# A two-layer trunk on one core: deeper ring, parts made earlier, and a hand order on ScalarE

## The chip, the cores and the metric

The kernel runs on one core of a Trainium2 chip. The metric is device time in microseconds (us), the median of several runs. The engines are TensorE (PE, its weight loads PEld), VectorE (DVE), ScalarE (ACT), GpSimd (POOL) and SyncE (SP), which here issues the transfers (DMA).

## The reference

256 tokens of 1024 float32 values go through two layers. Each layer is a mixer and a PEER expert retrieval, each followed by a layer norm over the residual:

```python
for i in range(2):
    m = mla(x) if i == 0 else dsa(x)
    x = layernorm(ALPHA * x + m, ln_gain[i, 0], ln_bias[i, 0])
    f = peer(x, w_q[i], sub_keys[i], w_down[i], w_up[i])
    x = layernorm(ALPHA * x + f, ln_gain[i, 1], ln_bias[i, 1])
```

`mla` is attention with low-rank queries, keys and values; `dsa` is attention in which an indexer picks 64 keys for each query. Both have 8 heads of 128. PEER is:

```python
q = (x @ w_q).reshape(T, 8, 2, 128)          # 8 heads, two halves
s1, s2 = scores of each half against its 128 sub-keys
v1, i1 = top_k(s1, 16); v2, i2 = top_k(s2, 16)
best, pos = top_k(v1[:, :, :, None] + v2[:, :, None, :], 16)
expert = i1 * 128 + i2 at pos; gate = softmax(best)
a = x . w_down[expert]                        # 16384 experts of 1024
y = sum over the chosen of gelu(a) * gate * w_up[expert]
```

## The kernel before, in words

**Weights in blocks.** All weights are cut into 604 blocks of 128x1024 float32 (512 KB), numbered in the order of use: 0 to 22 for `mla`, 23 to 38 for the first layer's query weights of PEER, 39 to 166 `down`, 167 to 294 `up`, 295 to 331 for `dsa` (its query heads are 308 to 315, its key heads 316 to 323), then 332 to 347, 348 to 475 and 476 to 603 for the second PEER. PEER computes the hidden unit of every expert for every token and multiplies it with a gate matrix that is zero where the expert was not chosen, so that no rows are gathered.

**High and low parts.** A float32 product is made of float16 parts: ACT makes the high part `hi` of a block (`Split.high`, L89), DVE the low part `lo` (`Split.low`, L98), and PE adds three products: hi by the high part `xh` of x, hi by its low part `xl`, and lo by `xh`. In some stretches one block in three or four is "pooled" (`Stream._pooled`): ACT scales the raw block in place (L164), casts it (L166), and POOL subtracts (L168).

**The stream.** `Stream` (L101) carries the blocks. A raw block is loaded into one of 6 slots of the pool `raws` by SP (L133), its two parts go into rings of `RING` = 6 slots each. `get` takes a block and splits up to `AHEAD` = 3 blocks further; it also loads `DMA_AHEAD` = 5 beyond these. `open` and `close` are the same in two halves, for the places where highs and lows are placed by hand: `open` makes the high part of the next block, `close` its low part. A slot is free once its last reader is done, so a load waits for the low part of an earlier block.

**Order.** Where nothing is said, a scheduler decides the order of each engine's queue from the program. Some of it is set by hand: `queue` (from `queue_of`) chains instructions of an engine in the order of the calls, and `chains[engine]` does so with everything that passes through `pe`, `dve` or `act`; `ws.act = act` puts the stream's own highs into ACT's chain. Each engine executes its queue in order.

**Ends of stages.** `finish` (L472) ends a stage. It takes the last output blocks, normalises the two token tiles (class `Norm`: sums L418, square L426, centre L431, scale L436 and L438, result L443), turns them on PE (class `Turned`, L459, tile names `xt`), splits them into `xh` and `xl`, and begins the next stage's matmuls in row form with the four blocks that it opens (`unit`; "hh" is hi by xh, "lh" lo by xh, "hl" hi by xl). In PEER these row results `qw` are the first four query units.

**PEER.** `peer` (L1049) unscales `qw` (L372, from `begun`) into rows, turns them (`qwT`, L1079, copy L1080), goes on with `queries` (tiles `pq`) and `scores` (tiles `ps`, copy L1102). DVE then chooses the 16 best by MAX8 and its companions (`top16`, L1105 to L1109), makes pairs, ranks them (L1161, L1168, with POOL L1164) and at last one-hot rows `hot` (L1240) and gates (POOL L1242, ACT L1246) in `prepare`; meanwhile PE runs through the `down` blocks (tiles `d`). `place` adds a group to the gate matrix (tiles `G`). There are 64 groups. A loop over pairs of `down` blocks prepares one or two groups a pair, as many as are needed to be done in time.

**dsa.** `turn_all` rotates heads: two copies on ACT (L633, L634), multiplications on DVE (L638, L642) and POOL (L635). The query heads 0 to 7 come first, then the key heads in pairs between the steps of `attention` (scores `s`). ACT is chained from the first key heads on; the chain is cut once within `attention`, before the first outputs are kept.

**The first block.** `first` (L1337) does block 0 in pieces while x arrives in two halves.

## Time and profile before

| what | value |
|---|---|
| median of 3 runs | 1729.37 us (1728.97 to 1731.33) |
| the profiled execution | 1731.02 us |
| its span | 1729.1 us |
| moved by DMA | 335.61 MB, 194 GB/s on average |
| granted clock of PE over the span | 0.998 |
| low parts on DVE (L98, blocks) | 571, 776.1 us |
| high parts on ACT (L89, blocks) | 570, 594.8 us |

A row of a timeline gives the start in us from the span's start, the duration, engine, line and operation, what is written and read, and in brackets the idle time of that engine just before, with what ended it. "x2" is two instructions in a row. The first matmul rows of a stretch overlap: one is issued every 0.11 or 0.22 us while each is under way for longer.

### The profile page before, as it was taken

Reading aid. Unit: us, or ns where it says so; the run is one execution under the profiler, and the core shown is the slowest. Engines: PE = TensorE matmul, PEld = TensorE weight load, DVE = VectorE, ACT = ScalarE, POOL = GpSimd, SP = SyncE. Lnnn points to the kernel's source line nnn. Section 1 sums busy time; section 2 is a strip of 40 time slices with the busy share of each in tenths; the row PEclk is TensorE's granted clock in tenths of the full one; section 3 lists DMA queues with packets and bytes.
Section 4 is the critical chain, followed back from the end, with each engine's and each line's share of the span. In section 5 each row is a group of like instructions: output and inputs, shape, how many; then the busy total and the mean of one; then the engine's idle time right before and its main releaser. Section 6 shows DMA issues by size and latency. Waiting matters only on the chain.

```text
span 1729.1 us, 33166 instructions
## 1 busy us (share of the span) xinstructions
PE 1702.9 (98%) x12497; PEld 1193.2 (69%) x12497; DVE 1346.9 (78%) x3033; ACT 1096.5 (63%) x1908; POOL 393.5 (23%) x257
## 2 busy tenths in 40 slices
PE   9999999999999999999998999999999999999998
PEld 7678888899984444444577698888999954444443
DVE  7679999989996566566687799999899966566565
ACT  7666556888875555555476756567888755555553
POOL 3011254555530000000022012444555400000000
PEclk9999999999999999999999999999999999999999
DMA  9445556655567666666564555566555576666662
GB/s 330 156 168 175 187 191 202 213 173 171 172 194 237 204 205 202 203 205 205 190 237 147 196 171 175 193 205 221 172 171 172 178 247 204 202 205 204 201 204 77
DMA packets 93483, 335.61 MB, mean 194 GB/s; under 512 B 10368, under 2 KB 11392, under 8 KB 93312
## 3 DMA queue, kind: packets, MB, share of 16 engines
q1 hardware_dynamic: 93024, 332.87, 59.4%
q8 instruction: 100, 1.64, 0.4%
q14 instruction: 71, 0.58, 0.1%
q10 hardware_dynamic: 288, 0.52, 0.1%
HBM read 329.16 MB, written 4.19 MB: 193 GB/s over the span
## 4 chain that ended last, share of the span: by engine, by line
PE 86%; DVE 7%; issue 3%; ACT 2%; DMA 1%; POOL 1%; DVEq 0%; SPq 0%; POOLq 0%; ACTq 0%
PE y L340 40%; PE d L340 33%; PE G L340 3%; DVE lo L98 2%; PE pq L340 2%; PE qw L340 1%; ACT hi L89 1%; PE v L340 1%; PE s L340 1%; PE o L340 1%; PE h L340 1%; DMA raw<-in_down 1%; PE ps L340 1%; PE q L340 1%; PE qi L340 1%
## 5 line engine op out<-in xcount | busy, mean ns | idle before, releaser
L98 DVE SCALAR_TENSOR_TENSOR lo<-raw,hi 128x1024 f16<-128x1024 f32 (+1 forms) x571 | 776.1, 1363 | 234.4 <-ACT hi L89 233.4
L89 ACT ACTIVATE hi<-raw 128x1024 f16<-128x1024 f32 (+1 forms) x570 | 594.8, 1051 | 294.3 <-PE y L340 183.3
L340 PE MATMUL d<-xh,lo 128*128 128x256 f16 x2048 | 558.3, 273 | 3.0 <-DVE lo L98 2.4
L340 PE MATMUL d<-xh,hi 128*128 128x256 f16 x2048 | 558.2, 273 | 0.0
L340 PE MATMUL d<-xl,hi 128*128 128x256 f16 x2048 | 558.2, 273 | 0.0
L340 PEld LDWEIGHTS <-hi 128*128 128x128 f16 x5016 | 488.5, 98 | 58.8 <-issue 1.8
L340 PEld LDWEIGHTS <-xh 128*128 128x128 f16 x2320 | 226.4, 98 | 270.6 <-ACT xh L89 2.4
L340 PE MATMUL y<-lo,xh 128*128 128x512 f16 x1088 | 326.3, 379 | 0.0
L340 PE MATMUL y<-hi,xh 128*128 128x512 f16 x1088 | 326.0, 379 | 0.0
L340 PE MATMUL y<-hi,xl 128*128 128x512 f16 x1088 | 325.6, 379 | 0.0
L340 PEld LDWEIGHTS <-lo 128*128 128x128 f16 x2508 | 245.4, 98 | 35.1 <-DVE lo L98 5.6
L1242 POOL TENSOR_TENSOR gate<-hot,gate 128x512 f16<-128x512 f16 x128 | 219.5, 1734 | 187.0 <-DVE hot L1240 187.0
L340 PEld LDWEIGHTS <-xl 128*128 128x128 f16 x1160 | 113.3, 98 | 138.2 <-DVE xl L98 2.5
L1246 ACT ACTIVATE gate<-hot,rest 128x128 f16<-128x128 f16 x512 | 165.9, 411 | 8.2 <-DVE hot L1240 8.2
L89 ACT ACTIVATE xh<-arena 128x512 f16<-128x512 f32 x131 | 82.0, 629 | 133.6 <-PE y L340 132.2
L98 DVE SCALAR_TENSOR_TENSOR xl<-arena,xh 128x512 f16<-128x512 f32 x134 | 91.9, 688 | 61.0 <-ACT xh L89 60.8
L168 POOL TENSOR_TENSOR lo<-raw,hi 128x1024 f16<-128x1024 f32 x26 | 58.1, 2234 | 192.2 <-ACT hi L166 150.8
L438 POOL TENSOR_TENSOR st<-st,mhalf 128x1 f32<-128x1 f32 x6 | 3.3, 556 | 414.2 <-DVE st L436 414.2
L164 ACT ACTIVATE raw<-raw 128x1024 f32<-128x1024 f32 x26 | 27.4, 1056 | 110.4 <-DMA raw<-in_down 91.0
L1164 POOL TENSOR_TENSOR arena<-arena 128x800 f32<-128x800 f16 x32 | 72.4, 2263 | 71.6 <-DVE arena L1161 63.4
L1240 DVE TENSOR_TENSOR hot<-iota,place 128x1024 f16<-128x1024 f16 x128 | 82.8, 689 | 6.4 <-PE G L340 3.9
L580 POOL TENSOR_SCALAR fit<-fit 128x2 f32<-128x2 f32 x1 | 0.2, 229 | 316.2 <-DVE junk L562 316.2
(210 smaller groups left out, 1578.3 us busy)
## 6 DMA issues: line engine op xcount, KB each, us to landing
raw<-in_down SPq DMA_DIRECT2D x256, 512.0 KB, 3.4
raw<-in_up SPq DMA_DIRECT2D x256, 512.0 KB, 4.2
raw<-in_peer_q SPq DMA_DIRECT2D x24, 512.0 KB, 4.6
raw<-in_dsa_qk SPq DMA_DIRECT2D x16, 512.0 KB, 4.6
raw<-in_mla_w_o SPq DMA_DIRECT2D x8, 512.0 KB, 5.3
arena<-in_peer_q SPq DMA_DIRECT2D x8, 512.0 KB, 4.9
raw<-in_dsa_v SPq DMA_DIRECT2D x8, 512.0 KB, 4.3
raw<-in_dsa_w_o SPq DMA_DIRECT2D x8, 512.0 KB, 3.8
```

Of the source, the lines that this page charges most:

```text
L89: return nc.scalar.copy(o, src) if unit == 1.0 else nc.scalar.mul(o, src, unit)
L98: return nc.vector.scalar_tensor_tensor(o, src, unit, hi, op0=ALU.mult, op1=ALU.subtract, accum_out=total)
L164: self.act(lambda: nc.scalar.mul(raw, raw, unit))
L168: nc.gpsimd.tensor_tensor(lo, raw, hi if short else hi.bitcast(F32), op=ALU.subtract)
L340: return pe(lambda: nc.tensor.matmul(o, l, r, start=start, stop=stop, skip_group_check=True))
L438: nc.gpsimd.tensor_tensor(st[:, 5:6], st[:, 4:5], mhalf, op=ALU.pow)
L580: nc.gpsimd.tensor_scalar(fit[:, 0:2], fit[:, 0:2], MOST * SMALL, None, op0=ALU.is_lt)
L1164: nc.gpsimd.tensor_tensor(o.rearrange("p k c -> p c k"), same, cell[t][:, h, :, None].to_broadcast([P, CELLS, TOPK]), op=ALU.mult)
L1240: nc.vector.tensor_tensor(hot, iota4[:, None].to_broadcast([P, 2, P, 4]), place16[:, :, None, four].to_broadcast([P, 2, P, 4]), op=ALU.is_ ...
L1242: nc.gpsimd.tensor_tensor(gate[:, 0], hot[:, 1].rearrange("p c j -> p j c"), gate16[:, four, None].to_broadcast([P, 4, P]), op=ALU.mult)
L1246: nc.scalar.mul(gate[:, 1, j, :], hot[:, 1, :, j], rest[:, t : t + 1])
```

## The change

- `RING` 6 to 8 and `AHEAD` 3 to 5: parts are made up to five blocks ahead. `raws` 6 to 4 and `DMA_AHEAD` 5 to 3: fewer raw blocks. The memory in all is the same.
- `stop=True` marks three places where the blocks of a stage end: splitting ahead does not run past them, as the next stage opens its blocks by hand.
- `finish`: the first three blocks are opened, and the first closed, ahead of the first norm; the fourth is opened ahead of the second norm's sums; the second low half of x comes before the centre of the second norm, which is cut into two halves around the scale; the first matmuls of the next stage come in another order.
- ACT's chain: it starts with the last two query heads in `dsa` and is not cut in `attention`; in `peer` it starts before the unscales, with the stream's highs in it, and ends after the first `queries`.
- The loop over `down` pairs prepares one group a pair at first and two at the end, where it was two at first.
- `first`: the high part of block 0 in two halves on ACT, its low parts ahead of x's, all of x's highs on ACT, and the matmuls piece by piece.

```diff
-RING = 6
+RING = 8
-    AHEAD = 3
-    DMA_AHEAD = 5
+    DMA_AHEAD = 3
+        self.AHEAD = 5 if split.short else 3
+        self.stops = []
...
     def _split(self, upto, pooled):
-        while self.n_split <= min(upto, len(self.blocks) - 1):
+        end = min([s for s in self.stops if s > self.n_taken], default=len(self.blocks))
+        while self.n_split <= min(upto, end - 1):
...
-    raws = pool("raws", 6 if short else 4)
+    raws = pool("raws", 4)
...
         n0, n1 = norms
+        blk = [ws.open(queue) for _ in range(3)]
+        ws.close(blk[0], queue)
         n0.sums()
...
         x0, x1 = Turned(queue, 0, spare[0]), Turned(queue, 1, spare[1])
-        blk = [ws.open(queue) for _ in range(3)]
+        blk.append(ws.open(queue))
         n1.sums()
         x0.high(0, 2)
         x0.high(1, 4)
         n1.square()
         x0.low(0)
-        n1.centre()
-        blk.append(ws.open(queue))
+        x0.low(1)
+        n1.centre(slice(0, 512))
         n1.scale()
-        x0.low(1)
+        n1.centre(slice(512, D))
         n1.result()
...
-        do(0, "hh", 0, 1, 2)
-        do(0, "lh", 0, 1, 2)
-        do(0, "hh", 3)
-        do(0, "lh", 3)
+        do(0, "hh", 0, 1, 2, 3)
+        do(0, "lh", 0, 1, 2, 3)
+        do(0, "hl", 0)
         x1.high(0, 2)
         x1.high(1, 4)
         do(1, "hh", 0, 1, 2, 3)
-        ws.close(blk[0], queue)
         ws.close(blk[1], queue)
         x1.low(0)
-        do(0, "hl", 0, 1)
+        do(0, "hl", 1)
...
         swap, cosine, total = meanwhile(6)
-        chains["act"] = None
...
         for h in range(0, HEADS, 2):
+            if h == HEADS - 2:
+                chains["act"] = None
+                ws.act = act
             turn_all(heads(qT, h))
...
-        ws.act = act
         turn_all(heads(kT, 0))
...
+        chains["act"] = None
+        ws.act = act
         for t, q in enumerate(begun.pop("q")):
-            unscale(qrow[t], q, unit)
+            act(lambda: unscale(qrow[t], q, unit))
...
         queries(4)
+        chains.pop("act")
...
-                want = min(64 - groups, -(-(64 - groups) // left))
+                want = min(64 - groups, 1 if 64 - groups <= 2 * (left - 1) else 2)
...
-        queue("act", lambda: split.high(hi0, raw0, W_UNIT))
-        x_high(0, "dve")
...
+        for i in range(2):
+            s = slice(512 * i, 512 * i + 512)
+            queue("act", lambda: split.high(hi0[:, s], raw0[:, s], W_UNIT))
         w_low(0)
-        x_low(3)
         w_low(1)
+        for c in range(4):
+            x_high(c)
+            last = x_low(c)
         busy(WARM, 512)
-        passes(hi0, xh, 0, 1)
...
+        for c in range(2):
+            passes(hi0, xh, c)
+            passes(lo0, xh, c)
+        passes(hi0, xl, 0, 1)
         busy(2)
+        for c in range(2, 4):
+            passes(hi0, xh, c)
+            passes(lo0, xh, c)
         passes(hi0, xl, 2, 3)
```

How the queues move is shown at three places. First ACT in `dsa`, from a high part of the key heads to the copies of the next keys, before. The numbers behind names are those of the tiles: q_10334 holds the last query heads, q_10402 the first key heads, raw_10438 is block 325:

```order
L89 ACTIVATE hi_10433<-raw_10271 128x1024
L164 ACTIVATE raw_10438<-raw_10438 128x1024
L89 ACTIVATE hi_10470<-raw_10302 128x1024
L633 COPY arena<-q_10334 64x512
L634 COPY arena<-q_10334 64x512
L89 ACTIVATE hi_10500<-raw_10340 128x1024
L89 ACTIVATE hi_10564<-raw_10370 128x1024
L633 COPY arena<-q_10402 64x512
L634 COPY arena<-q_10402 64x512
L89 ACTIVATE hi_10594<-raw_10407 128x1024
```

The same place on ACT in the changed kernel, where q_10342 holds the last query heads and q_10411 the first key heads:

```order
L637 COPY arena<-q_10342 64x512
L638 COPY arena<-q_10342 64x512
L89 ACTIVATE hi_10412<-raw_10310 128x1024
L89 ACTIVATE hi_10442<-raw_10348 128x1024
L637 COPY arena<-q_10411 64x512
L638 COPY arena<-q_10411 64x512
L89 ACTIVATE hi_10478<-raw_10379 128x1024
```

The scale of a pooled block (L164) is gone from here, the query copies stand one high earlier, and two highs, as before, lie between them and the copies of the keys.

Second, ACT at the start of the first PEER, before. hi_1167 and hi_1171 are blocks 29 and 30, raw_1175 is the pooled block 33; hi_1261 is 32:

```order
L89 ACTIVATE xh<-xt_1107 128x4x128
L89 ACTIVATE hi_1167<-arena 128x1024
L89 ACTIVATE hi_1171<-arena 128x1024
L164 ACTIVATE raw_1175<-raw_1175 128x1024
L89 ACTIVATE hi_1217<-raw_1137 128x1024
L372 ACTIVATE arena<-qw_1082 128x512
L372 ACTIVATE arena<-qw_1083 128x512
L89 ACTIVATE hi_1261<-raw_1147 128x1024
L166 CAST hi_1302<-raw_1175 128x1024
L1080 COPY arena<-qwT_1205 128x4x128
```

And the same place in the changed kernel; hi_1155 is block 27, and the highs that follow are 28 to 34 in order:

```order
L89 ACTIVATE xh<-xt_1110 128x4x128
L376 ACTIVATE arena<-qw_1083 128x512
L376 ACTIVATE arena<-qw_1084 128x512
L89 ACTIVATE hi_1155<-arena 128x1024
L89 ACTIVATE hi_1159<-arena 128x1024
L89 ACTIVATE hi_1163<-arena 128x1024
L89 ACTIVATE hi_1167<-arena 128x1024
L89 ACTIVATE hi_1173<-raw_1171 128x1024
L89 ACTIVATE hi_1179<-raw_1177 128x1024
L89 ACTIVATE hi_1225<-raw_1183 128x1024
L89 ACTIVATE hi_1269<-raw_1185 128x1024
L1087 COPY arena<-qwT_1213 128x4x128
```

The unscales (L372, now L376) stand ahead of the highs of blocks 27 to 34; before, those of 27 and 28 stood further up, ahead of the last turned tiles of x.

Third, DVE in the first `finish`, from the second norm's sums on, before:

```order
L421 TENSOR_SCALAR st<-st 128x1
L98 SCALAR_TENSOR_TENSOR xl,sums<-xt_1057,xh 128x4x128
L431 SCALAR_TENSOR_TENSOR arena<-arena,st 128x1024
L436 TENSOR_SCALAR st<-st 128x1
L98 SCALAR_TENSOR_TENSOR xl,sums<-xt_1064,xh 128x4x128
L443 SCALAR_TENSOR_TENSOR arena<-arena,st 128x512 x2
L98 SCALAR_TENSOR_TENSOR lo_1046,sums<-raw_927,hi_1045 128x1024
L98 SCALAR_TENSOR_TENSOR lo_1049,sums<-raw_929,hi_1048 128x1024
```

and in the changed kernel:

```order
L425 TENSOR_SCALAR st<-st 128x1
L98 SCALAR_TENSOR_TENSOR xl,sums<-xt_1060,xh 128x4x128
L98 SCALAR_TENSOR_TENSOR xl,sums<-xt_1067,xh 128x4x128
L435 SCALAR_TENSOR_TENSOR arena<-arena,st 128x512
L440 TENSOR_SCALAR st<-st 128x1
L435 SCALAR_TENSOR_TENSOR arena<-arena,st 128x512
L447 SCALAR_TENSOR_TENSOR arena<-arena,st 128x512 x2
L98 SCALAR_TENSOR_TENSOR lo_1038,sums<-raw_936,hi_1037 128x1024
```

The two low halves of x stand together ahead of the centre, the centre is in two pieces around the scale, and the first block's low part stands no longer here but ahead of the first norm's sums.

## The prediction

> **What bounds the kernel now.** I read the page first, for the share of each engine (busy time, share, instructions):

> ```profile
> PE 1702.9 (98%) x12497; PEld 1193.2 (69%) x12497; DVE 1346.9 (78%) x3033; ACT 1096.5 (63%) x1908; POOL 393.5 (23%) x257
> ```

> TensorE (PE) is busy 98% of a span of 1729.1 us, and no matmul is removed or added. So the change can win only time in which PE stands still, or runs at a lower clock. Next the busy time by stretches, to see where PE has gaps and where another engine is as full: a stretch with hidden and up blocks, and the selections of the two PEER layers (columns: stretch, its length, busy time and instructions of PE, PEld, DVE, ACT and POOL, then the granted clock, DMA share and GB/s):

> ```profile
> 330.00:840.00 510.00, 510.00 (x3422) 315.53 (x3420) 366.90 (x644) 318.31 (x590) 95.94 (x56) 1.00 0.62 195
> 115.38:307.36 191.98, 188.49 (x1716) 167.97 (x1715) 183.14 (x573) 114.45 (x146) 62.76 (x40) 1.00 0.55 185
> 993.28:1183.76 190.48, 189.60 (x1732) 169.38 (x1730) 179.17 (x574) 114.26 (x146) 64.28 (x41) 1.00 0.58 189
> ```

> From 330 to 840 us PE has no gap. In the selections both PE and VectorE (DVE) are nearly full. Third, the waits of PE, which name its gaps (total, times, longest):

> ```profile
> PE s L340 <- DVE arena L642: 4.6, 1, 4.6
> PE idle L1345 <- DVE iotac L293: 2.5, 1, 2.5
> PE d L340 <- DVE lo L98: 2.4, 3, 1.0
> PE G L340 <- POOL gate L1242: 1.8, 4, 0.5
> PE ps L340 <- ACT arena L372: 1.3, 1, 1.3
> PE qw L340 <- DVE xl L98: 1.3, 2, 0.8
> PE qwT L1079 <- ACT arena L372: 1.1, 1, 1.1
> ```

> That is 15.0 us in seven kinds. One wait stands out: the first scores `s` of the second layer's attention.

> **First keys.** Here is ScalarE (ACT) ahead of that wait, then DVE:

> ```profile
> 913.89 1.06 ACT L164 ACTIVATE raw<-raw 128x1024 f32<-128x1024 f32 x1 [8.15 <-DMA raw<-in_dsa_w_o]
> ...
> 919.14 0.58 ACT L633 COPY arena<-q 64x512 f32<-64x512 f32 x1
> ```

> ```profile
> 917.12 0.69 DVE L638 TENSOR_TENSOR arena<-q,arena 128x512 f32<-128x512 f32 x1 [4.08 <-ACT arena L634]
> ```

> ```profile
> 920.36 0.69 DVE L638 TENSOR_TENSOR arena<-q,arena 128x512 f32<-128x512 f32 x1 [1.19 <-ACT arena L634]
> 921.71 0.69 DVE L642 TENSOR_TENSOR arena<-arena 128x512 f32<-128x512 f32 x1 [0.66 <-POOL arena L635]
> ```

> ACT had the scale of a pooled block ahead of its next work, and that scale waited 8.15 us for a transfer. So the copies of the last query heads came late (DVE's 4.08), those of the first keys at 919.14, the rotation of the keys ended at 921.71 + 0.69 = 922.4, and `s`, for which PE stood ready 4.6 us before, started there. The clock shows a second price:

> ```profile
> 917.00:922.00 5.00, 0.85 (x8) 1.00 0.00 0
> 922.00:926.00 4.00, 3.54 (x15) 0.58 0.28 99
> ```

> After the gap the granted clock is 0.58 over 4 us. If PE would have been full there at 1.00, the loss is up to 4 x 0.42 = 1.7 us; PE also has a small wait in this stretch, so I take 1.2. The changed ACT order has no pooled scale there, and the keys' copies stand two highs behind the last query copies. PE stands from about 917.6, after the next heads' two blocks; at 24 matmuls of 0.109 for a block the first keys' own matmuls ended 5.2 us earlier, at about 912.4. Copies 1.2, rotation 0.69 + 1.27 (between the start of L638 at 920.36 and L642 there are 1.35) + 0.69: about 3.3, so ready at about 915.7 and in time, with 1.9 us to spare. DVE must have ended its key selection by then; it had nothing to do from 917.12 - 4.08 = 913.0 on before, and has the same work. Gain: 4.6 + 0.2 + 1.2 = **6.0 us**, between 4.6 (clock price elsewhere) and 6.5; nothing, if a transfer still holds ACT (a rival below).

> **Query rows.** Here the hand order adds a wait. On ACT, in the first layer (second: the same order):

> ```profile
> 106.05 1.07 ACT L372 ACTIVATE arena<-qw 128x512 f32<-128x512 f32 x2
> ```

> and on PE the end of the query rows, followed by the next heads' `pq`, a matmul every 0.11 us (first layer, then the end in the second):

> ```profile
> 102.04 0.59 PE L340 MATMUL qw<-hi,xl 128*128 128x512 f16 x2
> 102.47 0.27 PE L340 MATMUL pq<-xh,lo 128*128 128x256 f16 x1
> 102.58 0.27 PE L340 MATMUL pq<-xh,hi 128*128 128x256 f16 x1
> ```

> ```profile
> 982.71 0.59 PE L340 MATMUL qw<-hi,xl 128*128 128x512 f16 x2
> ```

> Before, the high part of the next block was ready early and PE ran into `pq` without a gap; it then waited for the late unscale (1.1 us, `qwT` of the waits). Now the two unscales come first and all highs of the next eight blocks are queued behind them, because they are one chain. An unscale can't start until the query rows' last matmul. So from 102.5 on: second unscale 0.53 (half of 1.07), high 1.05, low on DVE 1.2, and hand-overs of some 0.1: about 2.9 us in which PE does two matmuls. That is a **new gap of 2.9 us** per layer, instead of 1.1 + 1.3 (`qwT` and `ps`) in the first layer and none in the second.

> Whether it turns the clock down too is bounded by rows: after the `qwT` wait of 1.1 us the stretch from 115.38 shows 1.00, after 4.6 us there was 0.58. 2.9 lies between; I count none, and 1.2 per layer as the far end. [...]

> **Selections.** What a gap of PE is worth there depends on DVE, whose chain runs from the first MAX8 to the first one-hot rows, after which GpSimd (POOL) makes the gate (the last two rows group DVE's low parts in the first and the second selection, with the idle time before them):

> ```profile
> 115.38 0.29 DVE L1105 MAX8 arena<-arena 128x8 f32<-128x128 f32 x1 [6.05 <-ACT arena L1102]
> ```

> ```profile
> 308.13 3.43 POOL L1242 TENSOR_TENSOR gate<-hot,gate 128x512 f16<-128x512 f16 x2 [10.65 <-DVE hot L1240]
> ```

> ```profile
> L98 DVE SCALAR_TENSOR_TENSOR lo<-raw,hi 128x1024 f16<-128x1024 f32 x59 | 85.3, 1449 | 3.5 <-ACT hi L89 3.2 <-issue 0.2
> ```

> ```profile
> L98 DVE SCALAR_TENSOR_TENSOR lo<-raw,hi 128x1024 f16<-128x1024 f32 x60 | 81.3, 1359 | 5.2 <-ACT hi L89 5.2
> ```

> In the first layer the chain lasts 191.98, of which DVE is busy 183.14. It starts later now: ACT copies the scores only behind ten highs, two of which (blocks 35, 36) need a raw slot that is free once the low parts of 31 and 32 are done. Unscales and first high to 104.2, five lows of 1.22 to 110.4, a transfer of 4.6 (below), then a high, another, and a copy: about 117.7 instead of 115.38, which is 2.3 later. One more low falls into it (60 for 59, 1.4). Against that, the 3.5 us of idle before lows may go, since highs are made five blocks ahead. So the one-hot rows come 0.2 to 3.7 us later; in the middle 2. PE's own path gets 1.1 + 1.3 + some 2 (most of `d`'s 2.4) shorter and 2.9 longer, and so is no longer the later one. The waits of `G` (1.8 in both layers) shrink by about a half, as one group per pair is prepared at first where there were two. First layer: +2.4 to -1.5, I take **0**. Second layer: the chain starts 4.8 later (993.28, now 983.1 + 15), has one low less (-1.3), had 5.2 of idle before lows to give back, and `G` as above: +1 to -3, since PE's own new gap stands against the gain, I take **0**.

> **Norms.** With the next high parts, one low part and the second low half of x ahead of the second norm's centre, the wait of `qw` should go. Third norm, DVE and then PE:

> ```profile
> 963.95 0.69 DVE L418 SCALAR_TENSOR_TENSOR arena<-arena,y 128x512 f32<-128x512 f32 x1 [2.76 <-PE y L340]
> ```

> ```profile
> 971.62 1.28 DVE L431 SCALAR_TENSOR_TENSOR arena<-arena,st 128x1024 f32<-128x1024 f32 x1
> ```

> ```profile
> 972.88 0.68 DVE L98 SCALAR_TENSOR_TENSOR xl<-xt,xh 128x512 f16<-128x512 f32 x1
> ```

> ```profile
> 973.63 0.61 PE L340 MATMUL qw<-hi,xl 128*128 128x512 f16 x2 [0.76 <-DVE xl L98]
> ```

> The low half moves from behind the centre to its front: 1.28 + 0.15 earlier, more than the 0.76. What is late next is the second norm's result, by 0.6 and the second start of a halved centre (about 0.1); its transposes follow other matmuls now. For the two waits of `qw` (1.3) and small ones beside them I take 0.5, 0.2 and 0.9 in the three norms: **1.6 us**, between 0.8 and 2.2. The low part in front of the sums costs nothing while DVE waits for PE's last output block (2.76 us before the sums, L418); without that cover it would be 1.2 per norm. The stores of x on SP's queue now stand behind a raw load that waits for that low; they are read a stage later, so nothing.

> **First block.** ACT, DVE, PE:

> ```profile
> 7.71 1.15 ACT L89 ACTIVATE xh<-arena 128x512 f16<-128x512 f32 x2 [1.19 <-DMA arena<-in_xT]
> ```

> ```profile
> 10.21 0.69 DVE L98 SCALAR_TENSOR_TENSOR lo<-raw,hi 128x512 f16<-128x512 f32 x1
> ```

> ```profile
> 11.41 0.27 PE L340 MATMUL h<-xh,hi 128*128 128x256 f16 x1
> ```

> x's second half lands at 7.7 either way; its highs end at 8.9 and its lows at about 9.7. The low half of the weights at 10.21, now made before, no longer ends last. Some 0.3 of matmuls follow: block 1 starts at about 10.0 and not 11.4. I take **1.2**, between 0.3 and 1.6.

> **Ring and raws.** Eight ring slots for six cost nothing in themselves. Four raw slots for six put the load of block i+4 behind the low of block i:

> ```profile
> raw<-in_peer_q SPq DMA_DIRECT2D x24, 512.0 KB, 4.6
> ```

> A slot's round is a transfer of 4.6, high 1.05, low 1.2 to 1.45: 7.1 at most, and waits in two queues. Four blocks at 24 x 0.109 = 2.62 us of matmuls give 10.5. I price it at 0, covered by 3.4 us and by five finished blocks.

> **Sum.** 6.0 + 1.6 + 1.2 + 0 + 0 = 8.8 us. The profiled execution took 1731.02, 1.65 above the median of the runs, 1729.37. So 1722.2 for one like it, and 1720.6 as a median: **1720.5**.

> **Rivals.**
> *Selection pays in full.* Both one-hot chains start late and get no idle back: -1.5 and -3. Gain 4.3: 1725. For it: DVE is 95% busy there. Against: idle before lows that the deeper ring should cover. Chance 0.15.
> *The first keys still wait.* ACT's fixed order holds the copies behind highs whose raws, in four slots, come late; if the wait for `s` keeps 4 us or more, the gain is 8.8 - 6.0 = 2.8 at most: 1726.5. For it: 8.15 us of waiting for a transfer in this very place. Against: that wait was the pooled scale's, for a block five ahead. Chance 0.12.
> *DVE gets all its idle back*: +2.4 and +1 in the selections, 2.2 in the norms: 4.0 more, 1716.5. Chance 0.10.
> *Slower: the slot's round decides.* With four slots a pooled block always meets the same slot:

> ```profile
> L168 POOL TENSOR_TENSOR lo<-raw,hi 128x1024 f16<-128x1024 f32 x26 | 58.1, 2234 | 192.2 <-ACT hi L166 150.8
> ```

> ```profile
> L1164 POOL TENSOR_TENSOR arena<-arena 128x800 f32<-128x800 f16 x32 | 72.4, 2263 | 71.6 <-DVE arena L1161 63.4
> ```

> Its round is 4.6 + 1.06 + 1.04 + 2.23 = 8.9 of 10.5, and one operation of the selection ahead of it on POOL (2.26, the second row) makes 11.2. Over 10.5, ACT's queue, in which the scale stands, holds the other highs, and DVE idles. At 0.7 for each of some 20 pooled blocks in the two selections (26 in all) that is 14: 8.8 - 14, so 1734.5. Chance 0.11. What speaks against it: the five finished blocks ahead must be used up first.

> **How the numbers follow.** Forecast 0.52, its own range 1717 to 1724. About 0.2% (3.5 us) is what a measurement of this kernel can tell: under 1725.9 is faster, over 1732.8 slower. Faster: 0.52, 0.10, and most of the first rival: 0.74. Same: the second rival and the rest of the first, 0.16. Slower: 0.10. The range leaves out the slower rival and a little below: 1715 to 1727.5.

> **What would show it.** Right: no wait of `s` on DVE's L642 above 1 us and the clock at 1.00 there; a gap of 2.6 to 3.1 us in PE in front of `pq` in both layers; block 1 starting before 10.4; the first one-hot rows 0 to 4 us later after the query rows. Wrong: a wait of `s` of 3 us or more, a clock under 1.00 behind the query rows, or waits of DVE on highs in the selections above 6 us each, which would be the raw slots.

## The result, and the profile after

The changed kernel takes 1743.29 us (median of 5 runs, 1741.39 to 1750.18) beside 1729.49 for the one before (5 runs, 1728.97 to 1731.33): ratio 1.0089, 95% interval 1.0077 to 1.0100. It is slower by 13.8 us, where 8.8 us of gain had been forecast. The profiled execution took 1741.39, with a span of 1739.6.

The head of the page, then PE's waits:

```profile
PE 1707.0 (98%) x12495; PEld 1195.4 (69%) x12495; DVE 1348.7 (78%) x3037; ACT 1098.9 (63%) x1907; POOL 395.9 (23%) x256
```

```profile
PE il L344 <- DVE arena L984: 3.7, 1, 3.7
PE G L344 <- POOL gate L1250: 3.7, 4, 1.4
PE pq L344 <- ACT hi L89: 3.3, 2, 1.6
PE idle L1353 <- DVE iotac L297: 2.5, 1, 2.5
PE pq L344 <- DVE lo L98: 1.8, 2, 0.9
PE o L344 <- ACT arena L698: 1.7, 2, 1.4
PE s L344 <- DVE arena L646: 1.6, 1, 1.6
PE s L344 <- ACT arena L376: 1.6, 3, 0.7
PE qr L344 <- ACT arena L376: 1.3, 1, 1.3
```

The big wait of before, `s` on DVE's rotation, is down from 4.6 to 1.6. The forecast waits of `pq` are there (3.3 + 1.8 in two layers). But at the head stands one that nobody had named: `il`, the indexer's scores in the second layer; and `qr` in the first attention had no wait before. PE's busy time is 4 us longer for the same matmuls, and the granted clock over the span is 0.996 where it was 0.998 (0.002 of 1739.6 us is 3.5 us), so part of the loss is clock.

Where the 10.4 us between the last matmuls of the two traces come from is seen by the start of PE's work at a few places. The table gives how much later than in the kernel before each begins (us, negative is earlier; "rows end" is the start of the last `qw` matmul); the other columns are experiments that come below.

| start of | after | ring_back | back_no_qchain | early_dsa | early_both |
|---|---|---|---|---|---|
| `kn`, first attention | +1.6 | -1.0 | -1.6 | +2.2 | +0.3 |
| first `y` of its output | +2.9 | -1.4 | -2.0 | +3.5 | +1.8 |
| rows end, first PEER | +2.4 | -1.1 | -0.5 | +2.9 | +1.3 |
| first `G` | +3.6 | -2.1 | -4.8 | +6.6 | +4.2 |
| `qi`, indexer | +3.6 | -1.8 | -4.5 | +7.0 | +5.4 |
| `q`, query heads | +10.1 | -2.3 | -4.9 | +7.4 | +5.8 |
| first `s` of dsa | +7.1 | -6.3 | -8.3 | +4.6 | +3.0 |
| rows end, second PEER | +6.3 | -7.4 | -8.9 | +3.8 | +2.2 |
| second layer's first `G` | +11.1 | -4.4 | -10.5 | +7.2 | +3.6 |
| last matmul | +10.4 | -5.8 | -11.7 | +6.5 | +2.3 |

In the column "after", 6.5 us are lost between `qi` and `q`, and 4.8 between the second rows' end and its first `G`; the first keys win 3.0 up to `s`. PE's trace divides the 6.5: 3.6 are lost up to the first `il`, which waits 3.7, and 2.9 behind it, where the granted clock is 0.50 (columns: stretch, length, PE busy, clock, DMA share, GB/s):

```profile
885.60:892.43 6.83, 6.24 (x24) 0.50 0.79 268
```

ACT in the indexer, after, shows what was late there:

```profile
858.37 1.06 ACT L89 ACTIVATE hi<-raw 128x1024 f16<-128x1024 f32 x1 [3.10 <-DMA raw<-in_dsa_iq]
861.04 1.06 ACT L89 ACTIVATE hi<-raw 128x1024 f16<-128x1024 f32 x1 [1.61 <-DMA raw<-in_dsa_iq]
863.58 1.63 ACT L89 ACTIVATE hi<-raw 128x1024 f16<-128x1024 f32 x2 [1.48 <-DMA raw<-in_dsa_iq]
865.69 1.06 ACT L89 ACTIVATE hi<-raw 128x1024 f16<-128x1024 f32 x1 [0.48 <-DMA raw<-in_dsa_v]
868.09 1.06 ACT L89 ACTIVATE hi<-raw 128x1024 f16<-128x1024 f32 x1 [1.34 <-DVE lo L98]
870.92 1.06 ACT L89 ACTIVATE hi<-raw 128x1024 f16<-128x1024 f32 x1 [1.77 <-DMA raw<-in_dsa_v]
872.00 0.58 ACT L637 COPY arena<-qi 32x512 f32<-32x512 f32 x1
```

Six times in a row the engine waits, five of them for a transfer, and only behind that come the copies of `qi`, at 872.00. Before they came at 864.81:

```profile
864.81 0.58 ACT L633 COPY arena<-qi 32x512 f32<-32x512 f32 x1
```

The wait for the small copies is a wait for raw blocks, at one remove. The loads of the new stage, as SP's queue issued them (the first row is the four blocks that are opened by hand; other transfers are left out at the dots):

```profile
822.04 8.19 SPq L136 DMA_DIRECT2D raw<-in_dsa_v  x4
832.40 0.33 SPq L136 DMA_DIRECT2D raw<-in_dsa_iq  x1
...
853.89 0.33 SPq L535 DMA_DIRECT2D x<-arena  x1
855.07 3.84 SPq L136 DMA_DIRECT2D raw<-in_dsa_iq  x3
859.73 0.33 SPq L136 DMA_DIRECT2D raw<-in_dsa_ik  x1
860.84 6.10 SPq L136 DMA_DIRECT2D raw<-in_dsa_v  x4
```

One block behind the four opened ones is loaded at 832.40, when DVE has ended the low part of the first of the four (832.3), which the change places ahead of the first norm. The next load, at 855.07, comes after the store of x and the low part of the second opened block (853.78 to 855.00). So the stage began with one block beyond the four.

PE at the end of the query rows in the first PEER, after:

```profile
106.65 0.28 PE L344 MATMUL pq<-xh,hi 128*128 128x256 f16 x1 [1.63 <-ACT hi L89]
...
107.92 0.39 PE L344 MATMUL pq<-xh,lo 128*128 128x256 f16 x1 [0.88 <-DVE lo L98]
```

Behind a last `qw` at 104.64, the gap is 2.84 us beyond the usual spacing, in two parts of about 1.8 and 1.04 with two matmuls between them; 2.9 had been forecast. What had not is the clock behind it, further below.

### The profile page after: what moved, and what is told of

Read it like the earlier page. It is cut to its first block, busy times and chain, and to the rows that moved or that the text cites. A ratio compares the mean times of both kernels' runs of the same rounds, so it can differ in the third digit from the quotient of the medians.

```text
span 1739.6 us, 33250 instructions
## 1 busy us (share of the span) xinstructions
PE 1707.0 (98%) x12495; PEld 1195.4 (69%) x12495; DVE 1348.7 (78%) x3037; ACT 1098.9 (63%) x1907; POOL 395.9 (23%) x256
## 3 DMA queue, kind: packets, MB, share of 16 engines
q8 instruction: 100, 1.64, 0.4%
## 4 chain that ended last, share of the span: by engine, by line
PE 77%; DVE 12%; ACT 3%; DMA 3%; issue 3%; POOL 1%; DVEq 0%; POOLq 0%; ACTq 0%; SPq 0%
PE y L344 39%; PE d L344 28%; DVE lo L98 5%; PE G L344 3%; PE pq L344 2%; ACT hi L89 2%; DMA raw<-in_down 1%; DVE arena L1116 1%; DVE arena L1113 1%; PE qw L344 1%; DVE arena L1175 1%; DVE arena L1115 1%; DMA raw<-in_mla_h 1%; PE q L344 1%; DVE arena L1114 1%
## 5 line engine op out<-in xcount | busy, mean ns | idle before, releaser
L98 DVE SCALAR_TENSOR_TENSOR lo<-raw,hi 128x1024 f16<-128x1024 f32 (+1 forms) x572 | 777.4, 1362 | 236.6 <-ACT hi L89 235.6
L89 ACT ACTIVATE hi<-raw 128x1024 f16<-128x1024 f32 (+1 forms) x572 | 597.3, 1049 | 324.9 <-PE y L344 181.8
L89 ACT ACTIVATE xh<-arena 128x512 f16<-128x512 f32 x132 | 82.6, 629 | 133.2 <-PE y L344 132.1
L98 DVE SCALAR_TENSOR_TENSOR xl<-arena,xh 128x512 f16<-128x512 f32 x134 | 91.8, 688 | 60.9 <-ACT xh L89 60.8
L344 PE MATMUL G<-gate,hot 128*128 128x128 f16 x1024 | 68.3, 219 | 3.7 <-POOL gate L1250 3.7
## 6 DMA issues: line engine op xcount, KB each, us to landing
raw<-in_down SPq DMA_DIRECT2D x256, 512.0 KB, 3.5
raw<-in_up SPq DMA_DIRECT2D x256, 512.0 KB, 4.3
raw<-in_peer_q SPq DMA_DIRECT2D x24, 512.0 KB, 4.9
raw<-in_dsa_qk SPq DMA_DIRECT2D x16, 512.0 KB, 4.3
raw<-in_mla_w_o SPq DMA_DIRECT2D x8, 512.0 KB, 5.1
arena<-in_peer_q SPq DMA_DIRECT2D x8, 512.0 KB, 4.5
raw<-in_dsa_v SPq DMA_DIRECT2D x8, 512.0 KB, 4.5
raw<-in_dsa_w_o SPq DMA_DIRECT2D x8, 512.0 KB, 3.4
```

The source lines that it names most:

```text
L89: return nc.scalar.copy(o, src) if unit == 1.0 else nc.scalar.mul(o, src, unit)
L98: return nc.vector.scalar_tensor_tensor(o, src, unit, hi, op0=ALU.mult, op1=ALU.subtract, accum_out=total)
L344: return pe(lambda: nc.tensor.matmul(o, l, r, start=start, stop=stop, skip_group_check=True))
```

## The experiments

Beside every run stands the kernel before on the same chip (medians 1727.8 to 1728.3). A diff shows what a version changes in the changed kernel, or in the version that is named. Theories A and B are those of the next text, C and D are explained where the text asks why four slots hurt.

**Is it the stream or the hand order?** The stream as before, all hand orders kept:

```diff
-RING = 8
+RING = 6
-    DMA_AHEAD = 3
+    DMA_AHEAD = 5
-        self.AHEAD = 5 if split.short else 3
+        self.AHEAD = 3
-    raws = pool("raws", 4)
+    raws = pool("raws", 6 if short else 4)
```

> The changed kernel with the stream as before: six ring slots, six raw slots, splitting three blocks ahead, loads five beyond. All of the hand order stays. Theory A (four raw slots and five blocks ahead put highs that wait for a transfer ahead of ScalarE's other work; that cost 2.9 us in the first attention and 6.6 in the indexer of the second): both losses go, 1743.3 - 9.5, so 1732 to 1735, and the wait of il on DVE L984 (3.7 us) is gone. Theory B (the new hand orders delay those places): within 2 us of the changed kernel, 1741 to 1745, and the wait stays.

Measured: 1724.3 (10 runs, 1722.5 to 1726.2) beside 1728.2, ratio 0.9979 (0.9969 to 0.9988). The stream's numbers cost 19 us, and without them the change is a gain. The wait of `il` is gone. The time lies outside the ranges of both theories: A named the stream rightly, but its 9.5 us are only half of the 19.

The counterpart is the kernel before with `RING` 8, four raw slots, five ahead, loads three beyond, and the marked stage ends, and nothing else:

> The kernel before with the stream of the changed one alone: eight ring slots, four raw slots, splitting five ahead up to the marked stage ends, loads three beyond. No hand order is changed. Theory A: slower than before by the two losses of about 9.5 us, 1737 to 1741, with a wait of il of 2 us or more. Theory B: within 2 us of before, 1728 to 1731.

Measured: 1736.3 (6 runs, 1731.4 to 1743.1) beside 1728.2, ratio 1.0045 (1.0026 to 1.0063). The wait of `il` is there (2.9 us), and the median lies just under theory A's range, though the runs scatter over 12 us. The stream's numbers cost the kernel before 8.1 us and the changed one 19.0: the rest comes only together with the hand orders.

**Depth of splitting, slots, or distance of loads?** The changed kernel with three ahead (`self.AHEAD = 3`), eight ring and four raw slots:

> The changed kernel with eight ring slots and four raw slots, but splitting three blocks ahead. If the depth of splitting is what hurts (highs ahead in ScalarE's queue), most of the 9.5 us come back: 1733 to 1736. If the four raw slots alone hurt (a load waits for the low part of the block four before), it stays at 1741 to 1745 or gets worse. If the hand order is the cause: 1741 to 1745 as well, with the wait of il at 3.7 us.

Measured: 1743.6 (4 runs, 1740.9 to 1745.9) beside 1728.2, ratio 1.0095 (1.0076 to 1.0114): in the total nothing comes back, so how far ahead parts are made is not what costs the 19 us. The loss does move: in this trace the second rows end only 1.5 us later than before (6.3 in the changed kernel), but the wait of `pq` on ACT grows from 3.3 to 6.5, and at the first hidden units behind it the two are level again (11.5 and 10.8 later than before). Then `ring_back` with `DMA_AHEAD = 3`:

> As the version with the stream as before, but loads are issued only three blocks beyond the split parts; six raw slots stay. If the number of raw slots is what hurts: as with five, 1723 to 1726. If the earlier place of a load in the queue of SP is what hurts: half or more of the 19 us come back, 1733 or slower.

Measured: 1724.7 (10 runs), ratio 0.9979 (0.9969 to 0.9989), as with five. So the distance of the loads is not it either, which leaves the number of raw slots. (The two versions also differ in the ring slots, eight and six. No run has four raw slots beside six ring slots; that more ring slots do no harm is argued, not shown.) A point between, five raw and seven ring slots (`AHEAD` 4, `DMA_AHEAD` 4), without the chain at the query rows:

> The changed kernel without the chain at the query rows, with five raw slots and seven ring slots, four ahead. It stands between 1734.4 (four raw slots) and 1720.9 (six). Theory C: the fifth slot lets one block be loaded before the stage starts, and recovers a half or a little more: 1725 to 1729. Theory D (the slot's round, 8.9 us for a pooled block against 10.5 with four slots and 13.1 with five): with five the round is no limit, 1720 to 1723.

Measured: 1727.7 (10 runs), between 1734.4 for four (below) and 1720.9 for six, as theory C had it. And seven raw with five ring slots:

> The version with the stream as before and without the chain at the query rows (1720.9), with seven raw slots and five ring slots, three ahead. If raw slots are what the ends of stages run short of: no slower, 1718 to 1721. If six raw slots suffice and five ring slots delay the highs: 1722 or slower.

Measured: 1723.3 (9 runs), ratio 0.9973 (0.9963 to 0.9983): 2.4 us slower than six by the medians, though the intervals overlap. The trace shows waits of the x transposes on the second norm (6.4 us in four waits), and the first rows end 4.1 us later than before. By the medians six and six is the best of the four splits.

**Why do four slots hurt?** In the version with six the same loads look so:

```profile
826.19 5.51 SPq L136 DMA_DIRECT2D raw<-in_dsa_iq  x3
...
848.49 0.33 SPq L535 DMA_DIRECT2D x<-arena  x1
849.67 0.33 SPq L136 DMA_DIRECT2D raw<-in_dsa_iq  x1
851.43 0.33 SPq L136 DMA_DIRECT2D raw<-in_dsa_ik  x1
853.19 3.73 SPq L136 DMA_DIRECT2D raw<-in_dsa_v  x4
```

Of the four indexer blocks three had been loaded before the norms, and one in the other version. The theory that follows: at a stage's end the blocks opened by hand hold their raw slots until the norms are done, all but the first, whose low part is made early; with six slots three more blocks are there by then, with four slots one. Call this theory C; its rival, theory D, is that four slots are too few in steady running. To test it, the four blocks behind the opened ones get a place of their own, 70 us earlier, while the slots stay four:

```diff
+            if k == 100 and short and not last:
+                ws.ahead(299 - ws.n_taken, [arena[:, 15360 + i * D : 15360 + (i + 1) * D] for i in range(4)])
             if k == 64:
```

> The changed kernel (four raw slots) in which the four blocks behind those that the second layer opens by hand (299 to 302, the indexer's queries) are loaded some 70 us earlier into unused memory of their own. Theory C (the four opened blocks hold all four raw slots to the end of the norms, so the next stage starts with nothing loaded): the indexer's loss of about 7 us goes, 1743.3 - 6 to 7: 1735.5 to 1738.5, the wait of il on DVE L984 is under 1 us, and the rest of the loss (first attention, selections) stays. Theory D (four slots are too few in steady running): those four blocks only shift it, 1741 to 1744, with a wait of il of 2 us or more.

Measured: 1738.5 (4 runs, 1737.5 to 1740.1), ratio 1.0066 (1.0049 to 1.0082). The wait of `il` is gone, and from `qi` to `q` the trace loses 0.4 us instead of 6.5: theory C in this place, at the lower end of its gain (4.8 us by the medians). Its "nothing loaded" is one block by the rows above. The rest of the loss stayed. At the start of the kernel the same was tried with two blocks, which is what six slots would hold more:

```diff
     with tc.issue_after(last.ins):
         ws._load(3)
+        if short:
+            for i in range(4, 6):
+                ws.early[i] = arena[:, 22496 + i * D : 23520 + i * D]
+                nc.sync.dma_start(ws.early[i], ws.blocks[i][0])
```

> early_dsa with two more blocks (4 and 5) loaded early at the start of the kernel into unused memory. Theory C (at the start of a stage the slots are held, the next blocks come late): the start of kn moves 2 to 3 us forward against early_dsa, and the time falls by 3 to 4 us, 1734.5 to 1736. Theory D (steady running of four slots): kn moves by less than 1 us, 1737.5 to 1739.

Measured: 1735.5 (4 runs, 1733.4 to 1740.7), ratio 1.0052 (1.0032 to 1.0071). The median is theory C's, but with four runs the interval overlaps that of `early_dsa`, so here the trace has to carry the point. `kn` starts 1.9 us earlier than in `early_dsa`, a little under its 2 to 3. ACT's waits for transfers in the first attention, grouped, in the changed kernel (8 to 70 us) and in this one:

```profile
L89 ACT ACTIVATE hi<-raw 128x1024 f16<-128x1024 f32 x22 | 23.2, 1057 | 6.0 <-DMA raw<-in_mla_qk 2.3 <-DMA raw<-in_mla_h 1.5 <-DMA raw<-in_mla_w_o 1.0
```

```profile
L89 ACT ACTIVATE hi<-raw 128x1024 f16<-128x1024 f32 x20 | 21.0, 1058 | 3.3 <-DMA raw<-in_mla_qk 1.2 <-DMA raw<-in_mla_w_o 1.0 <-DMA raw<-in_mla_v 0.5
```

The idle time falls from 6.0 to 3.3. By the medians two stage starts explain 7.8 of the 19 us. Of the other 11 it stays open how they divide: in the column "early_both" against "ring_back" (8.1 us at the end, for the two executions profiled) they are spread over the rest of the first attention, the selections and the start of dsa, a few us each, and no run took one of these alone.

**The hand order at the query rows.** Undone in the changed kernel:

```diff
-        chains["act"] = None
-        ws.act = act
         for t, q in enumerate(begun.pop("q")):
-            act(lambda: unscale(qrow[t], q, unit))
+            unscale(qrow[t], q, unit)
...
-        chains.pop("act")
```

> The changed kernel without ScalarE's hand order at the start of PEER (the unscales of the query rows and the stream's highs are ordered by the scheduler again). Theory A says nothing of it: 1743.3 less the gap of 2.8 us in front of pq in each layer, plus what the late unscale costs again (1.1 us of qwT in the first layer): 1737 to 1740. If in the selections DVE's late start is what counts, 2 us more come back: 1735 to 1738. If the gaps are hidden by DVE anyway: 1742 to 1744.

Measured: 1734.4 (5 runs, 1734.0 to 1740.2) beside 1728.2, ratio 1.0049 (1.0031 to 1.0067): 8.9 us better than the changed kernel, a little more than any theory said, though the interval reaches into their ranges. The same with the stream as before:

> The changed kernel with the stream as before (six ring slots, six raw slots, three ahead) and without ScalarE's hand order at the start of PEER. Theory A2 (the chain at the query rows costs its gap of 2.8 us in both layers, whatever the raw slots): the version with the stream as before measured 1724.3; less 1.6 and 4.6 (what its way from the query rows to the first hidden units was longer than before), plus up to 2.8 for new waits of qw on the high parts of x, as there were in the changed kernel without the chain: 1718 to 1721. Theory B2 (the gaps count only beside four raw slots, DVE hides them otherwise): 1723 to 1725.

Measured: 1720.9 (5 runs, 1719.4 to 1722.2), ratio 0.9962 (0.9948 to 0.9976); theory A2. The chain costs 3.4 us beside six slots and 8.9 beside four. So 5.5 of the stream's 19 us come only together with this chain; without it four slots cost 13.5 (1734.4 to 1720.9). Or the chain stays and the next two blocks are made ahead of it:

```diff
+        ws.fill(ws.n_taken + 1)
         chains["act"] = None
```

> As the version with the stream as before, with ScalarE's hand order at the query rows kept, but the parts of the next two blocks (27, 28 in the first layer) are made ahead of the unscales, outside the chain. Theory A2: the two gaps in front of pq (1.6 + 1.0 us by the trace of the version with the stream as before) go and nothing else changes: 1724.3 - 2 x 2.8, so 1718 to 1720. Theory B2: 1723 to 1725. A rest above 1720 would say that the late copies of the scores, not the gap, cost the time.

Measured: 1721.9 (6 runs, 1720.6 to 1726.0), ratio 0.9968 (0.9956 to 0.9981): most of it, though not quite the 1718 to 1720. With the gaps gone, so is the lower clock behind them. That clock, in `ring_back` around the gap in the second layer and in `early2` at the same place (columns: stretch, length, PE busy, clock, DMA share, GB/s):

```profile
975.50:978.00 2.50, 0.83 (x5) 1.00 1.03 388
978.00:980.00 2.00, 1.16 (x6) 0.64 0.35 135
980.00:982.00 2.00, 2.00 (x12) 0.51 0.01 2
982.00:985.00 3.00, 3.00 (x30) 1.00 0.20 49
```

```profile
972.00:975.00 3.00, 3.00 (x23) 1.00 1.02 380
975.00:980.00 5.00, 5.00 (x48) 1.00 0.31 100
```

Twelve matmuls in 2 us at 0.51, where 2 us hold 18 or 19 of these at 1.00. From 978.84, where PE starts again, to 982.00 it issues 15, which take 1.64 us at 0.109 each: 1.5 us are lost on top of the gap's 2.84. Together 4.4, nearly all of what the way from the rows' end to the first hidden units is longer here (4.6).

**The first keys.** `ring_back` with ACT's chain in dsa as it was before (from the first keys on, cut in `attention`):

```diff
-            if h == HEADS - 2:
-                chains["act"] = None
-                ws.act = act
...
+        ws.act = act
         turn_all(heads(kT, 0))
...
         swap, cosine, total = meanwhile(6)
+        chains["act"] = None
```

> As the version with the stream as before, with ScalarE's chain in the second attention as it was (from the first keys on, cut before the first outputs). Theory of the prediction: the wait of s on DVE L642 (4.6 us) and the lower clock behind it are back, 5 to 6 us: 1729 to 1731. Rival: it was the raw slots or the order of the parts that ended that wait, and it stays away: 1723 to 1726.

Measured: 1730.6 (10 runs) beside 1728.3, 6.3 us slower than with the chain (1724.3). Its first wait, then the clock behind it:

```profile
PE s L344 <- DVE arena L646: 5.2, 1, 5.2
```

```profile
914.00:920.00 6.00, 0.78 (x8) 0.94 0.00 0
920.00:922.00 2.00, 2.00 (x7) 0.50 0.00 0
922.00:924.00 2.00, 2.00 (x10) 0.50 0.79 279
```

The wait of before is back, with its clock. The chain is the cause of the gain.

**The norms.** `back_no_qchain` with the whole of `finish` behind the norms' creation in the order of before:

> The version with the stream as before and without the chain at the query rows (1720.9), with the ends of the stages in the order of before. If the new order of the norms is worth the predicted 1.6 us: 1722 to 1723.5. If what it wins on the low half of x is lost again on waits for the high parts and for the second norm: 1720 to 1721.5. If it costs: 1718 to 1720.

Measured: 1718.9 (4 runs, 1718.2 to 1719.6), ratio 0.9948 (0.9932 to 0.9965). The new order wins nothing; the two intervals overlap and the spans of the profiled executions are 1717.5 and 1717.3, so that it costs is likely but not shown. PE's first wait in the first `finish` of `ring_back`, of `back_no_qchain` and of `old_finish`:

```profile
93.75 1.32 PE L463 MATMUL xt<-ident,arena 128*128 128x128 f32 x8 [0.73 <-DVE arena L447]
```

```profile
89.87 1.90 PE L344 MATMUL qw<-hi,xh 128*128 128x512 f16 x8 [1.32 <-ACT xh L89]
```

```profile
91.44 0.60 PE L344 MATMUL qw<-hi,xl 128*128 128x512 f16 x2 [0.54 <-DVE xl L98]
```

A wait of 0.54 on the low half of x is exchanged for one of 0.73 on the second norm's result, or of 1.32 on the high parts of x.

`old_finish` is also the version that beats both kernels: the one before, with the first block, the chain in dsa and the order of the gate groups of the change, and none of its stream (but the marked stage ends), query-row chain or norm order. It is 9 us faster than before, 24 faster than the changed kernel.

## Why the prediction was wrong, point by point

**Ring and raws: the step that failed.** "I price it at 0, covered by 3.4 us and by five finished blocks." Both covers are those of a stage that runs. At a stage's start there are no finished blocks beyond the four opened by hand, and the round of a slot there is not transfer, high and low, 7.1 us, but lasts until the norms let the lows come: the loads of the four blocks of the second layer were issued from 822.04 to 830.23, and three of their lows start at 853.78 and later. The slots had to be counted at the place where most of them are held. It cost 19.0 us (1743.3 to 1724.3), where 0 stood. Of these, 7.8 came back with room at two stage starts, and 5.5 come only together with the chain at the query rows; whether these shares overlap, and what the rest is, stays open. The sign that had been set down for the raw slots, waits of DVE on highs above 6 us in a selection, did not come (4.0 and 3.0 in the changed kernel): it looked at the wrong place.

**The slower rival** gave 1734.5 with a chance of 0.11 and had the right resource, but put its whole price on pooled blocks in the selections. In the selections the version with four slots lost 2.1 us more than `ring_back` on the way from the first hidden units to the first `G` of the first layer, and 2.0 in the second. In the first attention, where no block is pooled, it lost 4.3 more up to the first `y`, and in the indexer 7.0. Its question, whether five finished blocks would be used up, does not arise at a stage's start: they are not there yet.

**First keys: right.** 6.0 forecast, 6.3 measured by undoing it. In the changed kernel itself a wait of 1.6 remained: DVE's key selection ended at 923.7 and not, as had been counted on, at 913.0, and from there to the rotation of the first keys DVE had no idle time. (In the forecast, copies and rotation as written add up to 3.85 us and not to 3.3, as the first multiplication is counted twice; the 3.3 is right, by the 1.35 beside it.)

**Query rows: gap right, clock wrong.** 2.9 forecast, 2.84 in both layers of the changed kernel. I counted no loss of clock; that was an estimate between two waits, one of 1.1 us with 1.00 behind it and one of 4.6 us with 0.58. In three of four such gaps in the traces of the changed kernel and `ring_back` it fell (to 0.64 to 0.85, then 0.50 to 0.78); in the second layer of the changed kernel it stayed at 1.00. `dma3` keeps the same order at the query rows, and the granted clock over the span of its profiled execution is 0.999, as in `early2`, which has no wait of `pq`; in `ring_back` it is 0.997. So a gap of 2.84 us is not safe, and one need not cost clock either. Where the clock fell in `ring_back`, it cost about 1.5 rather than the 1.2 that I had put as the far end (more in the last section).

**Selections.** DVE's start in the first layer was right: 119.77 against a rows' end of 104.85 is 14.9 later, 15.2 had been worked out (117.7 less 102.5):

```profile
119.77 0.29 DVE L1112 MAX8 arena<-arena 128x8 f32<-128x128 f32 x1 [3.89 <-ACT arena L1109]
```

(The rows' end is the last `qw`, at 104.64, and its 0.21.) The one-hot rows follow 191.75 later (311.52) instead of 191.98, but not because idle time was given back, as I had assumed: DVE is idle for 9.3 us of this stretch, where it was 8.8, and its 60 low parts took 85.0 us, where 59 took 85.3. And in the second layer the new gap was not hidden: from the rows' end to the last matmul, 4.1 us were lost where I had put 0, though the clock stayed at 1.00 there.

**Norms: wrong, small.** 1.6 of gain forecast, none measured. I had named what is late next, and did not price it.

**First block: right.** 1.2 forecast; block 1 starts at 10.24 instead of 11.41, though no run took this part alone:

```profile
10.24 0.28 PE L344 MATMUL h<-xh,hi 128*128 128x256 f16 x1
```

With six slots the sum stands nearer: 8.8 forecast, 3.9 measured, and the 4.9 between are about the query rows (3.4) and the norms (1.6 that did not come).

## What to carry to other kernels

Count a buffer where most of it is held at once, not in steady running: at a stage's end, slots that wait for hand-placed work are no buffer, and the next stage starts nearly empty (here with one block beyond the four). A copy that ACT makes for PE waits for every transfer that the work ahead of it in the queue waits for (the copies of `qi` came at 872.00 where they had come at 864.81), so a lack of slots shows up as a wait on a small operation somewhere else. A chain that puts all later preparation behind one late instruction pays for its gap in time (2.84 us) and, behind three of four such gaps here, in clock as well (3.41 us at 0.50); two finished blocks ahead of it took the gap away here.

## What the runs showed of the hardware

```profile
103.95:107.36 3.41, 1.46 (x7) 1.00 1.02 381
107.36:110.78 3.42, 2.86 (x14) 0.50 0.22 87
988.00:991.41 3.41, 1.78 (x10) 1.00 1.03 375
991.41:994.83 3.42, 2.55 (x23) 1.00 0.40 157
```

In the first layer the gap left one step with 1.46 us of work, and the next step ran at 0.50. In the second it fell across two steps with 1.78 and 2.55, and the clock stayed at 1.00. In the traces of these two kernels, cut into such steps, the three steps at full clock that a half-clock step followed were busy for 0.00 (918.54, before), 0.43 and 0.08 of their time (103.95 and 882.19, after), and the least busy one that none followed for 0.52 (988.00, after; the start and the end of the kernel are left out). What happens between 0.43 and 0.52 was not shown, and no run moved one gap against the steps to test that it hangs on them.

Versions with four raw slots scatter more: 1741.4 to 1750.2 for the changed kernel (5 runs) and 1731.4 to 1743.1 for `ring_only` (6), against 1722.5 to 1726.2 for `ring_back` (10) and 1726.1 to 1731.3 for the kernel before (18), though `early_dsa` does not (1737.5 to 1740.1, 4 runs). No run shows what the scatter hangs on.
